# Two decoded rows on one set of partitions, and the mLSTM memory multiplied behind the last weight

## The chip, the cores and the metric

One core of a Trainium2 chip runs the whole program. The metric is device time in microseconds (us) for one execution. Five engines work side by side, each through its own instruction queue: PE (the matrix engine, with its weight loads shown apart as PEld), DVE (elementwise and reductions), ACT (activations and copies), POOL (a second, slower elementwise engine) and SP (no arithmetic; it issues DMAs). SP, ACT and POOL issue DMAs here.

## The reference, cut to what matters

One layer of a hybrid decoder runs on 256 prompt tokens and 8 decoded rows (264 columns in all): a combined projection, a gated recurrence and an mLSTM side by side, an output projection, cross-attention on 256 memory tokens, and a SwiGLU feed-forward. Two pieces of it are touched. The first is the new matrix memory of the prompt's four mLSTM heads:

```
w_end = jnp.exp(bcum[..., -1:] - bcum + li - m_new[..., None])
C_new = dec[..., None, None] * C + jnp.einsum('bhs,bhsd,bhsv->bhdv', w_end, kc, vc)
n_new = dec[..., None] * n + jnp.einsum('bhs,bhsd->bhd', w_end, kc)
```

The prompt's C starts at zero, so for each head the new memory is one product over the 256 tokens, of keys times weights (128 wide) with values and a column of ones (258 wide with padding). It is an output and nothing else in the layer reads it. The second piece is the attention of the 8 decoded rows, which read memory keys and values from a cache, 4 heads of 512 dimensions and 256 memory tokens:

```
s = jnp.einsum('blhd,bmhd->bhlm', xq, mk.astype(dt)).astype(jnp.float32) * (XA_DH ** -0.5)
p = jax.nn.softmax(s, axis=-1).astype(dt)
o = jnp.einsum('bhlm,bmhd->blhd', p, mv.astype(dt)).reshape(B, L, D_MODEL)
```

Each decoded row has keys and values of its own, so these products share no weights between rows.

## The kernel before, in words

The layer is a list `steps` of weight pieces: `w_in`, `w_out`, `w_q`, the memory's `w_k` and `w_v`, `w_o`, and the feed-forward's gate/up and down pieces. Each piece is loaded by SP in halves into one of five `raw` buffers, three pieces ahead. ACT then copies a half in a rounded matmul type into a `w` buffer (four of them), and DVE subtracts that copy from the original: high and low part of the weight. PE multiplies high by high, high by low and low by high, on 264 columns (line `mm<-B,w`). SP's order is the written one; on the other engines a scheduler places instructions by a simulated timeline, except for two stretches that are kept in written order.

Beside this main line run side generators, which `pump` advances between steps: the gates and heads of the mLSTM (`ml_gates`, `ml_prompt`, `ml_values`, `ml_heads`), the memory's norm, and the attentions. A `yield` with a number is a price by which the generators are paced. So their elementwise work stands between the weight splits on DVE and ACT.

In `ml_heads` each head multiplies `kw` (keys times weights) with `vt` (values) into a bank `cps`, 128x258 in plain fp32 and two matmuls for a head. ACT copies it to `cn`, and POOL's queue sends `cn` to the output `o_pc`.

The decode attention is `dec_k` and `dec_v`. A unit is one head and one row: 32 units. `dec_k` loads the row's keys, 128 partitions by 4 chunks of 256 tokens (512 KB), and the values alike, each into a fresh buffer of the pool `B` (26 buffers). The scores are a sum over 512 dimensions: ACT multiplies the first chunk by the query's column, DVE multiplies and adds the other three, ACT and POOL split the result in high and low (`ds`), and PE sums over the partitions by a matrix of ones (`onesr`), two matmuls for a unit, so that each partition holds every score. `dec_v` takes the maximum, the exponential and its sum, and multiplies the four value chunks by the weights with a running sum (`osm`). `NFL` lets two units be in flight.

The last step, `final(15)`, ends with three warm matmuls on ones whose result nobody reads (`warm(3)`). Then come sums of squares (`fin_sums`), the reciprocal root (`rstd_fin`: DVE, ACT's square root, and three more warm matmuls), two transpositions that spread it over the partitions (`spread`), and the products of the output with it, whose results SP and ACT send in nine pieces as `o_y`.

## Time and profile before

| what | before |
|---|---|
| median of 3 runs | 1457.74 us (1456.42 to 1458.74) |
| profiled execution, its own time | 1455.83 us |
| its span | 1454.11 us |
| granted clock of PE, mean | 0.998 |
| PE busy | 1439.2 us, 99% of the span |
| DVE, ACT, POOL busy | 1045.1, 794.9, 128.3 us |
| bytes moved | 326.02 MB, 224 GB/s on the mean |

The span counts from the first to the last instruction. PE's busy time contains overlaps, since matmuls are pipelined and their ends are modelled, so the distance from one start to the next says more of the price of a matmul than its duration. "Idle before, releaser" is the time an engine stood still ahead of a group, with what ended it.

### The profile page before, as it was taken

How to read it: one execution, taken by the hardware profiler on the slowest of the kernel's cores; microseconds unless marked ns; L12 is line 12 of the kernel's file. 1: busy time of each engine (PE TensorE's matmuls, PEld its weight loads, DVE VectorE, ACT ScalarE, POOL GpSimd, SP SyncE). 2: the span in 40 equal slices, each digit the busy share in tenths (PEclk: the TensorE clock that was granted, in tenths of full speed). 3: DMA queues.
4: the chain of work that ended last, by engine and by line, in shares of the span. 5: the costliest groups of instructions: out<-in, count | busy, mean ns of one | idle time of the engine just before them, and what ended most of it. 6: DMA issues, size and time to landing. Idle time of an engine off the chain costs nothing.

```text
span 1454.1 us, 30126 instructions
## 1 busy us (share of the span) xinstructions
PE 1439.2 (99%) x12071; PEld 1415.5 (97%) x12071; DVE 1045.1 (72%) x1999; ACT 794.9 (55%) x1279; POOL 128.3 (9%) x204
## 2 busy tenths in 40 slices
PE   9999999999999999999999999999999999999997
PEld 8999999999999999999999999999999999999997
DVE  7966797898899999987675666555665655565564
ACT  7678685666556666655544444434444443444463
POOL 0001210000124343410000000000000000000000
PEclk9999999999999999999999999999999999999999
DMA  9645896557799877955555555555555555555563
GB/s 288 234 171 179 268 363 231 177 178 271 254 344 355 340 284 297 375 172 192 197 195 194 197 193 201 190 202 190 198 194 196 196 198 194 195 197 192 172 195 112
DMA packets 99757, 326.02 MB, mean 224 GB/s; under 512 B 10944, under 2 KB 19824, under 8 KB 99616
## 3 DMA queue, kind: packets, MB, share of 16 engines
q1 hardware_dynamic: 83616, 269.84, 52.8%
q0 software_dynamic: 15136, 53.16, 10.2%
q8 instruction: 94, 1.54, 0.4%
q10 hardware_dynamic: 864, 1.09, 0.2%
q14 instruction: 47, 0.39, 0.1%
HBM read 312.78 MB, written 11.28 MB: 223 GB/s over the span
## 4 chain that ended last, share of the span: by engine, by line
PE 94%; ACT 2%; DMA 1%; DVE 1%; issue 1%; SPq 0%; POOL 0%; DVEq 0%; POOLq 0%
PE mm L60 90%; PE ax L60 5%; DMA raw<-w_in 1%; ACT B L60 1%; DVE B L60 1%; DMA B<-scr 0%; ACT w L60 0%; DVE w L60 0%; ACT L60 0%; SPq L213 0%; ACT dw L60 0%; DVE ds L60 0%; SPq L1412 0%; DMA scr<-lt 0%; ACT t L60 0%
## 5 line engine op out<-in xcount | busy, mean ns | idle before, releaser
L60 PE MATMUL mm<-B,w 128*128 128x264 f32 (+1 forms) x10960 | 1281.2, 279 | 2.5 <-DVE w L60 2.1
L60 PEld LDWEIGHTS mm<-B,w 128*128 128x128 f32 x10960 | 1260.6, 189 | 10.7 <-DVE w L60 2.4
L60 DVE TENSOR_TENSOR w<-raw,w 128x1024 fp32r<-128x1024 f32 (+1 forms) x522 | 625.4, 1200 | 312.9 <-ACT w L60 312.2
L60 ACT ACTIVATE w<-raw 128x1024 fp32r<-128x1024 f32 (+1 forms) x522 | 536.0, 1028 | 531.8 <-PE mm L60 370.8
L60 PE MATMUL mm<-w,B 128*128 128x512 f32 x384 | 86.5, 380 | 0.0
L60 PEld LDWEIGHTS mm<-w,B 128*128 128x128 f32 x384 | 70.7, 189 | 9.4
L1494 POOL TENSOR_TENSOR B<-B,rstd 128x264 f32<-128x264 f32 x4 | 2.8, 741 | 802.8 <-ACT rstd L60 802.8
L60 DVE TENSOR_TENSOR t<-mm,rstd 128x264 f32<-128x264 f32 x96 | 41.4, 432 | 28.8 <-PE mm L60 28.7
L60 DVE SCALAR_TENSOR_TENSOR B<-B,dw 128x256 f32<-128x256 f32 x128 | 52.2, 461 | 3.2 <-ACT dw L60 2.9
L60 DVE TENSOR_TENSOR xres<-xres,mm 128x264 f32<-128x264 f32 (+1 forms) x81 | 34.2, 424 | 27.2 <-PE mm L60 27.1
L60 DVE SCALAR_TENSOR_TENSOR dw<-B,qsm,dw 128x256 f32<-128x256 f32 x96 | 48.6, 512 | 0.8
L60 PE MATMUL ax<-B,B 128*128 128x256 f32 (+3 forms) x288 | 46.0, 302 | 0.8 <-DVE B L60 0.8
L1162 POOL TENSOR_TENSOR ds<-dw,ds 128x256 fp32r<-128x256 f32 x32 | 36.8, 1151 | 106.9 <-ACT ds L60 104.7
L60 PEld LDWEIGHTS ax<-B,B 128*128 128x128 f32 x288 | 39.9, 191 | 3.0 <-DVE B L60 1.0
L60 ACT ACTIVATE B<-xres,vecs 128x264 fp32r<-128x264 f32 (+1 forms) x64 | 32.1, 502 | 3.5 <-DVE xres L60 1.6
L60 ACT ACTIVATE t<-xres 128x264 f32<-128x264 f32 (+1 forms) x53 | 21.0, 409 | 16.0 <-DVE xres L60 16.0
L1151 POOL DMA_DIRECT2D B<-kcT x32 | 17.4, 544 | 122.8 <-DVE B L60 109.7
L60 DVE SCALAR_TENSOR_TENSOR B<-xres,vecs,B 128x264 fp32r<-128x264 f32 x48 | 23.3, 488 | 4.3 <-ACT B L60 4.3
L60 ACT ACTIVATE dw<-B,qsm 128x256 f32<-128x256 f32 x32 | 16.2, 507 | 16.3 <-issue 6.4
L60 ACT ACTIVATE B<-t 128x264 fp32r<-128x264 f32 (+1 forms) x60 | 24.1, 409 | 1.7 <-DVE t L60 1.5
L60 ACT ACTIVATE dw<-B,B 128x128 f32<-128x128 f32 x64 | 20.9, 390 | 7.1 <-DMA B<-scr 6.3
L60 ACT ACTIVATE dw<-ax,dw 128x256 f32<-128x256 f32 x32 | 15.0, 470 | 17.7 <-DVE dw L60 14.0
(172 smaller groups left out, 691.2 us busy)
## 6 DMA issues: line engine op xcount, KB each, us to landing
raw<-w_gu SPq DMA_DIRECT2D x176, 512.0 KB, 3.6
raw<-w_d SPq DMA_DIRECT2D x80, 512.0 KB, 3.7
raw<-w_in SPq DMA_DIRECT2D x74, 512.0 KB, 5.2
raw<-w_out SPq DMA_DIRECT2D x32, 512.0 KB, 3.8
B<-kcT POOLq DMA_DIRECT2D x32, 512.0 KB, 8.2
raw<-w_q SPq DMA_DIRECT2D x32, 512.0 KB, 5.4
B<-vcT POOLq DMA_DIRECT2D x32, 512.0 KB, 9.1
raw<-w_k SPq DMA_DIRECT2D x32, 512.0 KB, 5.1
```

The source lines that it names most:

```text
L60: return f(*a, **k)
L1151: pool_e.dma_start(kc, kcT[h, b])
L1162: pool_e.tensor_sub(ws[:, 1], acc, ws[:, 0].bitcast(F32))
L1494: e.tensor_mul(st["y"](c), st["y"](c), r)
```

## The change

The first part moves the mLSTM memory. Its eight matmuls, ACT's copies and the output leave `ml_heads`. Keys times weights now stand in one buffer for four heads (`kb`), and this and the two value buffers (`vts`) are written to DRAM by three DMAs of POOL's queue (512, 516 and 516 KB). At the fifth of the last sixteen weight pieces SP reads them back (`state_load`). The matmuls take the place of warm matmuls: head 0 in `final(15)`, head 1 in `rstd_fin`, heads 2 and 3 behind the spread. ACT copies the banks out (`state_out`), and `o_pc` is sent by SP in two halves, the first ahead of the first `o_y`, the second behind the last. PE's order in the last step is now the written one.

The second part puts two decoded rows on one set of partitions: each row takes 64 partitions and 8 chunks instead of 128 and 4, so that 16 units of two rows stand for 32 of one. `onesr` becomes two 64x64 blocks of ones with zeros beside them, and one matmul sums both rows. The queries come on the other partitions by a POOL copy and four DMAs of 64x16 elements for a head (`swap_q`), and results return in the same way (`swap_o`). Keys and values no longer take a fresh buffer for every unit: a `Ring` has two fixed tiles for keys and two for values, and a tile's next load is issued behind its fourth use.

```diff
...
-        warm(3, v[:, 0:1])
+        state_mm((1, 0), (1, 1))
         for k in "ps", "copied":
             fin[k] = bank("ax")
             spread(fin[k], [r[:, j: j + 1] for j in range(3)])
         act.activation(rstd, fin["copied"][:, :N], AF.Copy)
+        state_out(0, act)
+        state_out(1, act)
+        state_mm((2, 0), (2, 1), (3, 0), (3, 1))
+        state_out(2, act)
+        state_out(3, act)
 
...
         return f
 
     hT = {}
+    kept_k = drm.tile([P, H, 2, P], F32, name="kept_k")
+    kept_v = drm.tile([2, P, 2, 2, 258], F32, name="kept_v")
+
+    def state_load():
+        kb, vb, out = B([P, H, 2, P]), [B([P, 2, 2, 258]), B([P, 2, 2, 258])], B([P, H, 258])
+        sp.dma_start(kb, kept_k)
+        for q in range(2):
+            sp.dma_start(vb[q], kept_v[q])
+        fin["state"] = kb, vb, out
+        fin["cps"] = {}
+
+    def state_mm(*parts):
+        kb, vb, out = fin["state"]
+        for h, t in parts:
+            if t == 0:
+                fin["cps"][h] = bank("ax" if h % 2 else "mm")
+            pe.matmul(fin["cps"][h][:, 0:258], kb[:, h, t, :], vb[h // 2][:, t, h % 2, :],
+                      start=t == 0, stop=t == 1)
+
+    def state_out(h, engine):
+        out = fin["state"][2]
+        engine.activation(out[:, h, :], fin["cps"][h][:, 0:258], AF.Copy)
+
 
     def ml_prompt():
         qk = ml["qk"]
         yield STEP
-        kt = B([P, 2, H, P])
+        kt, ml["kb"] = B([P, 2, H, P]), B([P, H, 2, P])
...
-            w = B([P, 1024])
-            E, Pm, kw = w[:, 0:384], w[:, 384:768], w[:, 768:1024]
+            w = B([P, 768])
+            E, Pm, kw = w[:, 0:384], w[:, 384:768], ml["kb"][:, h].rearrange("p t d -> p (t d)")
             ml["w", h] = (Pm, kw)
...
 
     def ml_values():
         vts = [B([P, 2, 2, 258]), B([P, 2, 2, 258])]
+        ml["vts"] = vts
...
-        cn = B([P, H, 258])
...
-            cps = bank("ax")
-            pe.matmul(cps[:, 0:258], kw[:, 0:P], vt[:, 0, :], start=True, stop=False)
-            pe.matmul(cps[:, 0:258], kw[:, P:T], vt[:, 1, :], start=False, stop=True)
-            dps = cps[:, 300:302]
+            dps = bank("ax")[:, 0:2]
             for vb in range(2):
                 act.activation(hh(2 * h + vb)[:, 0:T], nps[:, vb * T: vb * T + T], AF.Copy)
             act.activation(den[:, 3 * h: 3 * h + 2], dps, AF.Abs)
-            act.activation(cn[:, h, :], cps[:, 0:258], AF.Copy)
-        pool_e.dma_start(o_pc, cn)
         yield STEP
 
...
             else:
-                warm(3)
+                state_mm((0, 0), (0, 1))
                 sq = tmp()
...
             if m == 0:
                 act.activation(warm_act, acc_x[:, 0:1], AF.Sqrt)
+            elif m == 4:
+                state_load()
             elif m == KC - 2:
...
             dve.tensor_mul(qsm[:, j, :], p2[:, 1, T - m:], rstd[:, T:N])
             qn["n"] = j + 1
+            if j % 4 == 3:
+                swap_q(j // 4)
             if j == 3:
                 with tc.issue_after(st["split"].ins):
-                    act.activation(onesr, ones, AF.Copy)
+                    act.activation(onesr, ones, AF.Copy, scale=0.0)
+                    for part in (LOW, HIGH):
+                        act.activation(onesr[part, part], ones[part, part], AF.Copy)
                 st["dk"] = side(dec_k(), 5)
                 st["dv"] = side(dec_v(), 4)
         return f
 
     pairs = []
     infl = {"n": 0}
+    NB2 = NS // 2
+    q2 = const.tile([P, H, 2, 4, NB2], F32, name="q2")
+    q3 = const.tile([P, 2, 2, 4, NB2], F32, name="q3")
+    o2, o3 = q2, q3
+    LOW, HIGH = slice(0, 64), slice(64, P)
+
+    by_row = lambda x: x.rearrange("p c (b s) -> p s c b", s=2)
+
+    def swap_q(h):
+        pool_e.tensor_copy(q3[:, h % 2], by_row(qsm[:, 4 * h: 4 * h + 4, :]))
+        for q, part in enumerate((LOW, HIGH)):
+            for e in range(2):
+                pool_e.dma_start(q2[part, h, e], q3[e: P: 2, h % 2, q])
+
+    def swap_o(h):
+        rec = ssm[:, h, 0: NB2]
+        dve.reciprocal(rec, rec)
+        o = o2[:, h].rearrange("p g c b -> p (g c) b")
+        dve.tensor_mul(o, o, rec.rearrange("p (c b) -> p c b", c=1).to_broadcast([P, 8, NB2]))
+        for q, part in enumerate((LOW, HIGH)):
+            for e in range(2):
+                pool_e.dma_start(o3[e: P: 2, h % 2, q], o2[part, h, e])
+        pool_e.tensor_copy(by_row(osm[:, 4 * h: 4 * h + 4, :]), o3[:, h % 2])
+
+    class Ring:
+        def __init__(self, src):
+            self.t, self.at = [B([P, 4, T]), B([P, 4, T])], 0
+            self.src = src.rearrange("h b p c t -> h (b p) c t")
+            self.load()
+            self.load()
+
+        def load(self):
+            u = self.at
+            if u < H * NB2 * 2:
+                self.at = u + 1
+                b = u // 2 % NB2 * 2 * P + u % 2
+                pool_e.dma_start(self.t[u % 2], self.src[u // NS, b: b + 2 * P - 1: 2])
+
+        def __call__(self, j):
+            return self.t[j // 4][:, j % 4, :]
 
     def dec_k():
+        kr = Ring(kcT)
+        st["vr"] = Ring(vcT)
+        yield STEP
         for h in range(H):
             while qn["n"] < 4 * h + 4:
                 yield STEP
-            for b in range(NS):
+            for b in range(NB2):
                 while infl["n"] >= NFL:
                     yield STEP
                 infl["n"] += 1
-                kc = B([P, 4, T])
-                pool_e.dma_start(kc, kcT[h, b])
                 w = sb.tile([P, 264], F32, tag="dw", bufs=2, name=nm("dw"))
                 ws = sb.tile([P, 2, T], F32R, tag="ds", bufs=2, name=nm("ds"))
-                vc = B([P, 4, T])
-                pool_e.dma_start(vc, vcT[h, b])
                 acc = w[:, 0:T]
-                q = [qsm[:, 4 * h + c, b: b + 1] for c in range(4)]
-                act.activation(acc, kc[:, 0, :], AF.Copy, scale=q[0])
-                for c in range(1, 4):
-                    dve.scalar_tensor_tensor(acc, kc[:, c, :], q[c], acc, op0=OP.mult, op1=OP.add)
+                for j in range(8):
+                    q = q2[:, h, j // 4, j % 4, b: b + 1]
+                    if j == 0:
+                        act.activation(acc, kr(0), AF.Copy, scale=q)
+                    else:
+                        dve.scalar_tensor_tensor(acc, kr(j), q, acc, op0=OP.mult, op1=OP.add)
+                    if j % 4 == 3:
+                        kr.load()
+                    if j == 3:
+                        yield 1.0
                 act.activation(ws[:, 0], acc, AF.Copy)
                 pool_e.tensor_sub(ws[:, 1], acc, ws[:, 0].bitcast(F32))
-                pairs.append((h, b, w, vc, ws))
+                pairs.append((h, b, w, ws))
                 yield 1.1
 
     def dec_v():
         done, cur = 0, None
-        while done < H * NS:
+        while done < H * NB2:
             nxt = None
             if pairs:
                 nxt = pairs.pop(0)
                 ps = bank("ax")
-                pe.matmul(by2(ps[:, :T]), onesr, turn(nxt[4][:, 0]), start=True, stop=False)
-                pe.matmul(by2(ps[:, :T]), onesr, turn(nxt[4][:, 1]), start=False, stop=True)
+                pe.matmul(by2(ps[:, :T]), onesr, turn(nxt[3][:, 0]), start=True, stop=False)
+                pe.matmul(by2(ps[:, :T]), onesr, turn(nxt[3][:, 1]), start=False, stop=True)
                 nxt += (ps,)
             cur, todo = nxt, cur
             if todo is None:
                 yield STEP
                 continue
-            h, b, w, vc, _, ps = todo
+            h, b, w, _, ps = todo
             mx, p = w[:, T: T + 1], w[:, :T]
             dve.tensor_reduce(mx, ps[:, :T], axis=AX.X, op=OP.max)
             dve.tensor_scalar(mx, mx, -XSCALE, None, op0=OP.mult)
             act.activation(halves(p), unturn(ps[:, :T]), AF.Exp, scale=XSCALE, bias=mx,
                            accum_out=ssm[:, h, b: b + 1])
             yield 0.5
-            for c in range(4):
-                dve.scalar_tensor_tensor(vc[:, c, :], vc[:, c, :], 1.0, p, op0=OP.mult, op1=OP.mult,
-                                         accum_out=osm[:, 4 * h + c, b: b + 1])
+            for j in range(8):
+                v = st["vr"](j)
+                dve.scalar_tensor_tensor(v, v, 1.0, p, op0=OP.mult, op1=OP.mult,
+                                         accum_out=o2[:, h, j // 4, j % 4, b: b + 1])
+                if j % 4 == 3:
+                    st["vr"].load()
+                if j == 3:
+                    yield 1.0
             infl["n"] -= 1
             done += 1
-            if done % NS == 0:
-                dve.reciprocal(ssm[:, h, :], ssm[:, h, :])
-                for c in range(4):
-                    dve.tensor_mul(osm[:, 4 * h + c, :], osm[:, 4 * h + c, :], ssm[:, h, :])
+            if done % NB2 == 0:
+                swap_o(h)
+                yield STEP
                 st["dh"] = h + 1
             yield STEP
 
...
+        if i == len(steps) - 1:
+            kept.enter_context(tc.manual_schedule(engines={mybir.EngineType.PE}))
...
+        if i == 44:
+            pool_e.dma_start(kept_k, ml["kb"])
+            for q in range(2):
+                pool_e.dma_start(kept_v[q], ml["vts"][q])
     for e, x in pend:
         e(x)
+    kept.close()
     for lo, hi in ((0, 1), (1, 2), (2, 4), (4, 6), (6, 8), (8, 10), (10, 12), (12, 14), (14, 16)):
         for c in range(lo, hi):
             e, r = (pool_e, rstd) if c in POOLC else (dve, fin["ps"][:, :N])
             e.tensor_mul(st["y"](c), st["y"](c), r)
+        if lo == 0:
+            sp.dma_start(o_pc[:, 0:2], fin["state"][2][:, 0:2])
         (act if lo in (1, 4, 8, 12) else sp).dma_start(o_y[:, lo:hi, :], st["y"].tile(lo // 4)[:, lo % 4: lo % 4 + hi - lo, :])
+    sp.dma_start(o_pc[:, 2:4], fin["state"][2][:, 2:4])
```

On PE, in the last head of `ml_heads`, the rows before are these (`ax` with number 2083 is the bank `cps`, `B_1626` the buffer with keys times weights, `B_1889` the values):

```order
L60 MATMUL ax_2078<-B_1889,B_1626 128x256
L60 MATMUL ax_2078<-B_1889,B_1626 128x128
L60 MATMUL ax_2083<-B_1626,B_1889 128x258 x2
L60 MATMUL ax_2083<-ones,B_1889 128x1 x3
L60 MATMUL mm_2128<-B_148,w_2006 128x264
```

and at the same place of the changed kernel:

```order
L60 MATMUL ax_2082<-B_1893,B_1630 128x256
L60 MATMUL ax_2082<-B_1893,B_1630 128x128
L60 MATMUL ax_2087<-ones,B_1893 128x1 x3
L60 MATMUL mm_2129<-B_152,w_2010 128x264
L60 MATMUL mm_2129<-B_153,w_2010 128x264
```

The two matmuls of 258 columns are gone, and the weight's next matmul stands directly behind the three sums.

On PE, from the last weight matmuls to the end of the program, before (`c` is the small tile of the reciprocal root, `ident` the identity of the spread):

```order
L60 MATMUL mm_17732<-B_16571,w_17683 128x264
L60 MATMUL mm_17769<-ones 128x128 x3
L60 MATMUL ax_17728<-ones,t_17773 128x1 x3
L60 MATMUL mm_17791<-ones,c_17782 128x128 x3
L60 MATMUL ax_17795<-ident,c_17783 128x128 x2
L60 MATMUL ax_17795<-ident,c_17783 128x8
L60 MATMUL ax_17799<-ident,c_17783 128x128 x2
L60 MATMUL ax_17799<-ident,c_17783 128x8
```

and of the changed kernel (`B_17018` holds `kept_k`, `B_17019` and `B_17020` the halves of `kept_v`):

```order
L60 MATMUL mm_17545<-B_16375,w_17494 128x264
L60 MATMUL mm_17582<-B_17019,B_17018 128x258 x2
L60 MATMUL ax_17539<-ones,t_17585 128x1 x3
L60 MATMUL ax_17603<-B_17019,B_17018 128x258 x2
L60 MATMUL ax_17606<-ident,c_17595 128x128 x2
L60 MATMUL ax_17606<-ident,c_17595 128x8
L60 MATMUL ax_17610<-ident,c_17595 128x128 x2
L60 MATMUL ax_17610<-ident,c_17595 128x8
L60 MATMUL mm_17617<-B_17020,B_17018 128x258 x2
L60 MATMUL ax_17620<-B_17020,B_17018 128x258 x2
```

Heads 0 and 1 stand where the warm matmuls stood, heads 2 and 3 behind the spread.

On DVE, early in the decode attention, before (`dw` is a unit's scores, `B_5470` its keys, the rows with `w` are weight splits):

```order
L60 TENSOR_TENSOR w_5488<-raw_5374,w_5488 128x8x128
L60 SCALAR_TENSOR_TENSOR dw_5472<-B_5470,qsm,dw_5472 128x256
L60 TENSOR_SCALAR dw_5388<-dw_5388 128x1
L60 SCALAR_TENSOR_TENSOR dw_5472<-B_5470,qsm,dw_5472 128x256 x2
L60 TENSOR_TENSOR w_5570<-raw_5456,w_5570 128x8x128
L60 SCALAR_TENSOR_TENSOR B_5390,osm<-B_5390,dw_5388 128x256 x4
```

and of the changed kernel, at one of the closest places between two uses of a key tile (`B_5225` and `B_5226` are the two key tiles of the ring, `q_117` the turned queries):

```order
L60 SCALAR_TENSOR_TENSOR dw_7242<-B_5226,q_117,dw_7242 128x256
L60 TENSOR_TENSOR w_7715<-raw_7624,w_7715 128x1024
L60 SCALAR_TENSOR_TENSOR dw_7467<-B_5225,q_117,dw_7467 128x256
L60 TENSOR_TENSOR w_7768<-raw_7690,w_7768 128x1024
L60 SCALAR_TENSOR_TENSOR dw_7467<-B_5226,q_117,dw_7467 128x256 x2
L60 TENSOR_TENSOR w_7771<-raw_7692,w_7771 128x1024
```

The first row is unit `dw_7242`'s last use of the second key tile, which is then loaded again; the fifth row is the next unit's first use of it. Two weight splits and one product stand between them. Before, every unit's keys have a buffer of their own.

On SP, the end of the queue of the changed kernel; before, only the `o_y` rows stand there:

```order
L1581 DMA o_pc<-B_17021 128x516
L1582 DMA o_y<-B_16806 128x264
L1582 DMA o_y<-B_16806 128x528
L1582 DMA o_y<-B_17016 128x528
L1582 DMA o_y<-B_17232 128x528
L1582 DMA o_y<-B_17441 128x528
L1583 DMA o_pc<-B_17021 128x516
```

The two halves of the new memory enclose the five pieces of the output.

## The prediction

> **What bounds the kernel now.** I read the page's busy shares and slices first, then the waits of PE.
>
> ```profile
> span 1454.1 us, 30126 instructions
> PE 1439.2 (99%) x12071; PEld 1415.5 (97%) x12071; DVE 1045.1 (72%) x1999; ACT 794.9 (55%) x1279; POOL 128.3 (9%) x204
> PE mm L60 <- DVE w L60: 2.1, 2, 1.9
> PE ax L60 <- ACT w L60: 2.1, 3, 1.5
> PE mm L60 <- DVE ones L60: 1.1, 1, 1.1
> PE ax L60 <- DVE B L60: 0.8, 1, 0.8
> ```
>
> PE is busy for 99% of the span, and its named waits (total, times, longest) are about 6 us in all. So the kernel is a row of matmuls, and a matmul taken out of the dense part is worth its distance to the next start, as long as the weights still arrive in time. The span is 1454.11 us and the profiled execution 1455.83, so 1.72 us lie around it; the execution stands 1.91 us under the median of 1457.74.
>
> Next are the stretch of the decode attention, by windows (start:end, length, busy times of PE, PEld, DVE, ACT and POOL, clock, share of the DMA engines, GB/s), and a stretch of the feed-forward for comparison:
>
> ```profile
> 398.00:625.00 227.00, 227.00 (x1468) 210.87 (x1466) 220.02 (x564) 144.55 (x271) 88.95 (x121) 1.00 0.87 326
> 735.00:1000.00 265.00, 265.00 (x2358) 265.00 (x2357) 158.17 (x192) 115.81 (x133) 0.00 (x0) 1.00 0.56 195
> ```
>
> PE never waits in the decode stretch, but DVE is busy for 220.02 of 227 us. It has 7 us to spare there, and 107 of 265 in the feed-forward. That scarcity is where this change can go wrong.
>
> **What the matmuls that go are worth.** Starts and lengths of groups on PE, in the mLSTM and in the decode attention:
>
> ```profile
> 165.73 1.03 PE L60 MATMUL ax<-B,B 128*128 128x258 f32 x4
> 166.60 0.72 PE L60 MATMUL ax<-ones,B 128*128 128x1 f32 x6
> 461.81 0.28 PE L60 MATMUL ax<-ds,onesr 128*128 128x256 f32 x1
> 461.93 2.78 PE L60 MATMUL mm<-B,w 128*128 128x512 f32 x16
> L60 PE MATMUL ax<-B,B 128*128 128x258 f32 x16 | 4.2, 388 | 0.8 <-DVE B L60 0.8
> L60 PE MATMUL ax<-ds,onesr 128*128 128x256 f32 x64 | 17.1, 277 | 0.0
> ```
>
> A head's new memory is four records, from 165.73 to the next group's start at 166.60: 0.87 us, and four heads 3.5. A sum over the ones takes from 461.81 to 461.93, 0.12 us (0.11 where I averaged neighbouring starts). 64 become 32: 32 x 0.115 = 3.65 us. Both stand in stretches in which PE hardly waits, and the order on PE around them stays, so I take both whole: -7.15 us. The first heads wait for DVE's `B` (0.8 us in the row); that wait belongs to the keys and stays. ACT's four copies `cn` and POOL's `o_pc` go without worth, as ACT is busy for 55%.
>
> **What DVE and ACT get in the decode attention.** Groups between 375 and 655 us (count, busy, mean ns, idle before):
>
> ```profile
> L60 DVE TENSOR_TENSOR w<-raw,w 128x1024 fp32r<-128x1024 f32 x94 | 120.7, 1287 | 10.8 <-ACT w L60 10.5
> L60 DVE SCALAR_TENSOR_TENSOR dw<-B,qsm,dw 128x256 f32<-128x256 f32 x96 | 48.6, 512 | 0.8
> L60 DVE SCALAR_TENSOR_TENSOR B<-B,dw 128x256 f32<-128x256 f32 x128 | 52.2, 461 | 3.2 <-ACT dw L60 2.9
> L60 DVE TENSOR_REDUCE dw<-ax 128x1 f32<-128x256 f32 x32 | 13.3, 416 | 0.3 <-PE ax L60 0.2
> L60 DVE TENSOR_SCALAR dw<-dw 128x1 f32<-128x1 f32 x32 | 4.7, 147 | 0.2
> L60 ACT ACTIVATE w<-raw 128x1024 fp32r<-128x1024 f32 x94 | 99.0, 1055 | 39.5 <-PE mm L60 30.5 <-issue 5.1 <-DMA raw<-w_v 2.1
> L60 ACT ACTIVATE dw<-B,qsm 128x256 f32<-128x256 f32 x32 | 16.2, 507 | 16.3 <-issue 6.4 <-DVE B L60 4.7 <-ACT w L60 2.9
> L1162 POOL TENSOR_TENSOR ds<-dw,ds 128x256 fp32r<-128x256 f32 x32 | 36.8, 1151 | 106.9 <-ACT ds L60 104.7
> L1151 POOL DMA_DIRECT2D B<-kcT x32 | 17.4, 544 | 122.8 <-DVE B L60 109.7
> ```
>
> The multiply-adds on keys go from 96 to 112 (8 chunks for 16 units, less ACT's first): +16 x 0.512 = +8.2 us. Value products stay 128. Maxima and scalings halve: -16 x (0.416 + 0.147) = -9.0 us, and 16 small products at the heads' ends become four, at about the scaling's price, -12 x 0.147 = -1.8. DVE gains 2.6 us in all. ACT loses half of its first products (-16 x 0.507 = -8.1 us) and half of its copies and exponentials besides. POOL's subtractions fall by 16 x 1.151 = 18.4 us; its 32 new small DMAs cost 32 issues of 0.544 us, 17.4. None of this is on PE's path by itself, and it counts zero. What hides it is that the splits run ahead as far as their four buffers allow: ACT's copies stand idle for 30.5 us until PE releases a buffer, against 2.1 for a weight's DMA. If that cover went, every late us of DVE would be a us of PE.
>
> **The turned queries and results.** Each head's queries go through a POOL copy, four DMAs of 4 KB and their landing. The trace has no such small transfer on this queue; the nearest is a full key tile alone, at 3.8 us (below). For the first head this delays the first unit by 0 to 6 us, and later heads' queries are ready ahead. The attention ends some 24 us earlier in the changed order against PE's weight steps, which pays for the return of the results too. I take 0.
>
> **The ring.** Landing times, issue to data, of the 512 KB transfers (KB each, median us), of two single key tiles, at 581 us with nothing ahead of it and at 596.8 with several, and of the outputs in this stretch:
>
> ```profile
> raw<-w_d SPq DMA_DIRECT2D x80, 512.0 KB, 3.7
> raw<-w_v SPq DMA_DIRECT2D x32, 512.0 KB, 6.8
> B<-kcT POOLq DMA_DIRECT2D x30, 512.0 KB, 8.4
> B<-kcT POOLq DMA_DIRECT2D x1, 512.0 KB, 3.8
> ...
> B<-kcT POOLq DMA_DIRECT2D x1, 512.0 KB, 9.9
> ...
> o_k<-t POOLq DMA_DIRECT2D x16, 128.0 KB, 6.2
> o_v<-B POOLq DMA_DIRECT2D x8, 256.0 KB, 4.9
> ```
>
> Before, each unit had buffers of its own, and loads ran ahead. Now a tile is loaded behind its last use, and has until its next use. I added up DVE's durations from the trace over the changed order between these two points, for 61 reloads. Most have 9 to 20 us; fourteen have 2.9 to 7.9, nearly all of the second key tile. The place in the order shown above has two splits and one product: 2 x 1.287 + 0.512 = 3.1 us, 3.6 with the issue. The shortfall, summed over the reloads, is 4 us if a tile lands in 5, 11 at 6.5, 22 at 7.5 and 38 at 8.7. Against it stand DVE's 7 us and the 2.6 it gains. The ends are thus 0 (at 5, the tile alone) and 28 (at 8.7). I take a landing of 6.3, nearer the tile alone, because the second key tile is mostly asked for 2 to 7 us behind the last value tile and not in bursts of six. The shortfall is then about 10 us, DVE's spare is 9.6, and I count +1 us for the unevenness.
>
> The rate that the stretch needs: the weights' 195 GB/s (row of the feed-forward), 60 tiles (31.5 MB) of keys and values in about 218 us, 144, and the memory's keys and values written out (16 x 128 and 8 x 256 KB), 19: 358. One slice of 36 us of the page reached more:
>
> ```profile
> GB/s 288 234 171 179 268 363 231 177 178 271 254 344 355 340 284 297 375 172 192 197 195 194 197 193 201 190 202 190 198 194 196 196 198 194 195 197 192 172 195 112
> ```
>
> The slice with 375 says that the DMA can carry it, with 4% left. The Trainium skill, page "DMA: Bandwidth & Descriptors", section "Specifications", puts the limit of HBM for a core at about 358 GB/s, and this would leave nothing and keep landings at their burst level; by that rule the time would be the first rival's. The slice of 375 disagrees with the figure, so I keep the row.
>
> **The state's way through DRAM.** POOL's three writes (1.57 MB) stand on a queue whose engine is busy for 9% of the span. SP's three reads stand between weight loads of the last step's piece 4, where a weight half lands in 3.7 us and the DMA is at 56%. At 396 GB/s (the tail's row below) they take 4 us. SP runs as far ahead as five half buffers allow: a down piece of 12 chunks has 36 matmuls of 265 / 2358 = 0.112 us, 4.05 us, so two and a half pieces are 10 us, and 4 more on a queue that needs 3.7 still fit. I take 0, with 0 to 1.4 us as bounds (4 + 2 x 3.7 for two halves behind all three, less 10).
>
> **The tail.** The chain after the last weight matmul, from the timeline, and two windows of its end:
>
> ```profile
> 1441.56 0.83 PE L60 MATMUL mm<-ones 128*128 128x128 f32 x6
> 1442.45 0.83 PE L60 MATMUL ax<-ones,t 128*128 128x1 f32 x6
> 1443.32 0.16 DVE L60 TENSOR_SCALAR c<-ax 128x3 f32<-128x3 f32 x1 [1.06 <-PE ax L60]
> 1443.52 0.20 ACT L60 ACTIVATE c<-c 128x3 f32<-128x3 f32 x1 [0.51 <-DVE c L60]
> 1444.57 1.41 PEld L60 LDWEIGHTS ax<-ident,c 128*128 128x128 f32 x12 [0.29 <-DVE c L60]
> 1445.90 4.71 SPq L1495 DMA_DIRECT2D o_y<-B  x5
> 1448.00:1450.00 2.00, 0.00 (x0) 0.00 (x0) 1.61 (x5) 0.00 (x0) 1.44 (x3) 0.92 1.03 387
> 1450.00:1452.50 2.50, 0.00 (x0) 0.00 (x0) 0.00 (x0) 0.00 (x0) 0.00 (x0) 0.50 1.04 396
> ```
>
> Head 0 takes 0.87 us from 1441.56 and ends at 1442.43, when the sums start at 1442.45. Head 1 fits between the sums' end, 1443.3, and the spread at 1444.57. ACT copies head 0 out at about 1443.0 to 1443.45, just ahead of the square root at 1443.52. These cost 0, at most 0.2. Heads 2 and 3 run behind the spread, on a PE that has nothing else. The DMA then is saturated from 1448 to 1452.5. The first half of `o_pc` (264 KB) is asked for some 1 us ahead of the first `o_y`, while the DMA idles: 0. The second is last in the queue: 264 KB at 396 GB/s, +0.67 us. Bounds: 0, and 1.36 if both halves wait behind the output.
>
> **Sum.** 1455.83 - 3.5 - 3.65 + 1.0 (ring) + 0.67 (last half) = 1450.35 for the profiled execution; on the median, 1.91 higher, 1452.3, 0.38% less than before.
>
> **Rivals.**
>
> 1. *The ring's tiles come late* (slower; 0.25). DVE stands at the first use of a tile, the splits behind it on DVE come late, and PE with them. For it: DVE's 97%, the median landing of 8.4, 358 GB/s. Against it: single tiles at 3.8. It decides for "slower" when the loss passes 9.5 us, at a landing of about 7.3 (19 us of shortfall less 9.6); at 8.7 the loss is 28, 1479. Middle: about 1462.
> 2. *The tail pays more* (0.12). State copies delay the square root and ACT's share of the output's DMAs, and both halves queue: +2 to +3 us instead of 0.67, about 1454.
> 3. *PE's gain comes back as waits* (0.08). The splits run at DVE's pace in the decode stretch, so PE waits for the us that it saves there: only the mLSTM's 3.5 us stay or less, 1455 to 1458. Against it: 5 us of split slack, and DVE gains 2.6 of the 3.65.
>
> **How the numbers follow.** My forecast has 0.55 and its own range is 1449.5 to 1454.8: the low end is the sum without ring and tail, 1455.83 + 1.91 - 7.15 = 1450.6, less 1.1 for scatter of the medians; the high end adds a us or two of ring and tail. The whole range takes in rivals 2 and 3 and the lower half of the first, to 1464. A measurement of this kernel tells about 0.2%, 2.9 us, from no change. Faster: 0.53 from the forecast, 0.08 from rival 2, 0.01 from the others, 0.62. Same: 0.02, 0.04, 0.06, and 0.04 from a ring that loses 4 to 9 us, 0.16. Slower: 0.22, nearly all the ring's.
>
> **What would show it.** The two groups of matmuls must be gone, the mLSTM ending about 3.5 us earlier and the first feed-forward step 6 to 7. Right on the ring: PE without waits from 375 to 655, key tiles landing in about 6 us, and DVE with little idle ahead of `dw<-B,q` products. Wrong: DVE idle released by `B<-kcT` and PE waiting for `w`. The tail is right if the span behind the last weight matmul is 0.5 to 1 us longer.

## The result, and the profile after

The changed kernel takes 1482.31 us (median of 4 runs, 1478.93 to 1484.0) against 1457.55 us of the kernel before beside it (4 runs): a ratio of 1.0169, with a 95% interval of 1.0157 to 1.0182. It is slower by 25 us where I forecast 5 us faster. The profiled execution took 1482.38 us, its span is 1480.7.

First the page of the changed kernel, then its waits of PE over the whole span (total, times, longest):

```profile
span 1480.7 us, 29940 instructions
PE 1444.0 (98%) x12027; PEld 1413.9 (95%) x12027; DVE 1046.7 (71%) x1971; ACT 773.6 (52%) x1217; POOL 134.2 (9%) x230
```

```profile
PE ax L60 <- ACT ds L60: 8.0, 5, 4.6
PE mm L60 <- DVE w L60: 5.2, 6, 1.9
PE ax L60 <- DVE B L60: 4.0, 3, 1.7
PE mm L60 <- DVE t L60: 3.5, 1, 3.5
PE ax L60 <- POOL ds L1236: 2.7, 3, 1.6
```

PE's busy time has hardly moved; its waits have grown from some 7 to 29 us. Where they stand is told by comparing the two traces matmul by matmul. Both have the same 11,344 matmuls on weights, so the n-th of one answers to the n-th of the other. The changed kernel is 1.7 us ahead when the decode attention begins (at 375 us), 25.7 behind when it ends (at 660), and 25.7 behind at the last weight matmul. These rows show the lead at 303 us (303.25 - 301.58), and then the last weight matmul, each of before and then of the changed kernel:

```profile
303.25 0.59 PE L60 MATMUL ax<-lt,ones 128*128 128x256 f32 x2
```

```profile
301.58 0.59 PE L60 MATMUL ax<-lt,ones 128*128 128x256 f32 x2
```

```profile
1441.14 0.58 PE L60 MATMUL mm<-B,w 128*128 128x264 f32 x3
```

```profile
1466.82 0.58 PE L60 MATMUL mm<-B,w 128*128 128x264 f32 x3
```

From 660 us on nothing more is lost until the last weight: 1466.82 - 1441.14 = 25.68. What follows the last weight matmul is 0.88 us longer. So the span's 26.6 us are -1.7 (start and mLSTM), +27.4 (decode attention) and +0.9 (tail).

The decode stretch of the changed kernel, by windows as in the prediction, then its groups on DVE and ACT (count, busy, mean ns, idle before them), then its DMA issues (KB each, median us to landing):

```profile
398.00:625.00 227.00, 206.19 (x1290) 187.38 (x1290) 202.85 (x513) 111.37 (x191) 82.05 (x128) 0.98 0.87 302
```

```profile
L60 DVE SCALAR_TENSOR_TENSOR dw<-B,q,dw 128x256 f32<-128x256 f32 x112 | 58.4, 527 | 24.5 <-DMA B<-kcT 17.1 <-ACT dw L60 6.8 <-DVE w L60 0.2
L60 DVE SCALAR_TENSOR_TENSOR B<-B,dw 128x256 f32<-128x256 f32 x128 | 54.1, 483 | 1.8 <-DMA B<-vcT 1.1 <-ACT dw L60 0.6
L60 ACT ACTIVATE dw<-B,q 128x256 f32<-128x256 f32 x16 | 8.2, 510 | 43.4 <-DMA B<-kcT 22.8 <-DVE B L60 10.3 <-DVE w L60 4.8
```

```profile
B<-kcT POOLq DMA_DIRECT2D x30, 512.0 KB, 7.3
B<-vcT POOLq DMA_DIRECT2D x30, 512.0 KB, 6.2
```

PE, which was never idle there, is busy for 206 of 227 us. DVE waits 17.1 us for key tiles, and ACT 22.8 more. Key tiles land in a median 7.3 us, less than the 8.4 of before. So they are not slower; they are asked for later.

One such wait from end to end, in the changed kernel's timeline of DVE, POOL, ACT, DVE and PE (start, length, engine, work, idle before it and what ended it):

```profile
548.67 0.47 DVE L60 SCALAR_TENSOR_TENSOR dw<-B,q,dw 128x256 f32<-128x256 f32 x1
...
552.55 0.54 POOL L1206 DMA_DIRECT2D B<-kcT  x1 [7.84 <-ACT w L60]
...
561.60 0.51 ACT L60 ACTIVATE dw<-B,q 128x256 f32<-128x256 f32 x1 [7.57 <-DMA B<-kcT]
562.01 0.40 ACT L60 ACTIVATE ds<-dw 128x256 fp32r<-128x256 f32 x1
562.32 1.04 ACT L60 ACTIVATE w<-raw 128x1024 fp32r<-128x1024 f32 x1
...
562.21 1.36 DVE L60 SCALAR_TENSOR_TENSOR dw<-B,q,dw 128x256 f32<-128x256 f32 x2 [3.98 <-ACT dw L60]
...
562.46 0.58 PE L60 MATMUL ax<-ds,onesr 128*128 128x256 f32 x1 [4.62 <-ACT ds L60]
```

DVE's last product on the first key tile ends at 549.14. POOL asks for the next keys only at 552.55, 3.4 us later (its row names a weight split on ACT as what it waited for; which need of the load that stands for was not settled), and they land after 8.9 us more. Of the 30 reloads, 24 are asked for within 0.7 us of the last product on their tile, and six 1.1 to 3.4 us behind it. ACT stands for 7.57 us before its product on it. Behind that product in ACT's queue are the copy `ds` of the unit before, for which PE stands 4.62 us, and the next weight split. So ACT's wait for one unit's keys holds up another unit's sums.

### The profile page after: what moved, and what is told of

Same layout as the page of the kernel before. It is cut to its first block, busy times and chain, and to the rows that moved or that the text cites. A ratio compares the mean times of both kernels' runs of the same rounds, so it can differ in the third digit from the quotient of the medians.

```text
span 1480.7 us, 29940 instructions
## 1 busy us (share of the span) xinstructions
PE 1444.0 (98%) x12027; PEld 1413.9 (95%) x12027; DVE 1046.7 (71%) x1971; ACT 773.6 (52%) x1217; POOL 134.2 (9%) x230
## 4 chain that ended last, share of the span: by engine, by line
PE 57%; DMA 1%; DVE 1%; issue 0%; DVEq 0%; ACT 0%
PE mm L60 56%; PE ax L60 1%; DMA B<-vcT 1%; DMA B<-kcT 1%; DVE B L60 0%; DVE w L60 0%; DVE dw L60 0%; DVE c L60 0%; DVEq L1667 0%; DVE t L60 0%; ACT c L60 0%; DVEq L60 0%
## 5 line engine op out<-in xcount | busy, mean ns | idle before, releaser
L60 DVE SCALAR_TENSOR_TENSOR dw<-B,q,dw 128x256 f32<-128x256 f32 x112 | 58.4, 527 | 24.5 <-DMA B<-kcT 17.1
L60 ACT ACTIVATE dw<-B,q 128x256 f32<-128x256 f32 x16 | 8.2, 510 | 43.4 <-DMA B<-kcT 22.8
L60 ACT ACTIVATE dw<-B,B 128x128 f32<-128x128 f32 x64 | 20.7, 392 | 12.8 <-DMA B<-scr 11.2
L60 PE MATMUL ax<-B,w 128*128 128x264 f32 x144 | 22.2, 281 | 2.1 <-ACT w L60 2.0
L60 PEld LDWEIGHTS ax<-B,w 128*128 128x128 f32 x144 | 19.3, 189 | 3.2 <-ACT w L60 3.0
```

Of the source, the lines that this page charges most:

```text
L60: return f(*a, **k)
```

## Experiments

The theories are RING (two key tiles leave no time to land), RATE (the DMA can't carry the shorter stretch), SWAP (the small DMAs of queries and results clog POOL's queue) and, later, SCORES (too few score tiles). "Decode stretch" below is the difference to before between 375 and 660 us, matmul by matmul.

**e1, the first part alone.**

The decode attention is that of before, with one row for a unit and a buffer for every unit. The mLSTM memory, `state_load`, `state_mm`, `state_out` and `o_pc` are as in the change.

> Only the first part: the mLSTM memory behind the last weight matmul; the decode attention is that of before. By the alignment of the two traces (equal weight matmuls compared) this part gains 1.7 us in the mLSTM and loses 0.9 behind the last weight matmul, the decode attention has the whole loss: 1456.8 us, ratio 0.9995. If instead the DRAM traffic of the state were what disturbs the decode stretch, this kernel would be slower than before by some us.

Measured: 1455.7 us, ratio 0.9991 (0.9981 to 1.0). The mLSTM gains 4.1 us, the decode stretch loses 1.55 although its code is the same (the order shifted a little), and the tail loses 0.89. PE's waits between 375 and 655 us are a single row:

```profile
PE ax L60 <- POOL ds L1187: 0.2, 1, 0.2
```

The state's way through DRAM does not cost the decode stretch its 27 us; the loss is the second part's.

**e2, fresh tiles for every unit.**

```diff
-        kr = Ring(kcT)
-        st["vr"] = Ring(vcT)
...
+                kc = [half(kcT, h, b, u) for u in range(2)]
+                vc = [half(vcT, h, b, u) for u in range(2)]
```

> Both parts, but each unit of two rows takes fresh tiles of the pool for its keys and values and asks for all four at once at its start, as before; the ring of two tiles is gone. Theory RING (two key tiles leave no time to land): the 27 us of the decode stretch vanish and the 3.65 us of the sums come through, 1451 to 1457 us. Theory RATE (the DMA can't carry keys, values and weights in the shorter stretch): no better than 1475. Theory SWAP (the small DMAs and copies of the turned queries hold POOL's queue): no better than 1475.

Measured: 1468.36 us, 1.0083 (1.0067 to 1.01). Half of the loss comes back, and the decode stretch still loses 15 us. The forecast of RING is missed by 11 us. Nine of them are one stall, in the waits of PE, and its cause is in POOL's timeline:

```profile
PE ax L60 <- POOL ds L1223: 9.1, 1, 9.1
```

```profile
454.42 0.53 POOL L1191 DMA_DIRECT2D q<-q  x1 [1.73 <-DMA B<-kcT]
456.98 0.52 POOL L1191 DMA_DIRECT2D q<-q  x1 [2.03 <-DMA B<-kcT]
459.54 0.52 POOL L1191 DMA_DIRECT2D q<-q  x1 [2.04 <-DMA B<-vcT]
...
469.79 0.55 POOL L1182 DMA_DIRECT2D q<-q  x1 [1.96 <-DMA B<-vcT]
...
471.51 0.74 POOL L1223 TENSOR_TENSOR ds<-dw,ds 128x256 fp32r<-128x256 f32 x1
```

Eight small DMAs of 4 KB each wait 1.5 to 2.3 us, seven of them for an older key or value load by their rows, and the subtraction that PE needs stands behind them. The loads themselves are slow here: asked for in bursts, eight of them land one every 2.55 us, 12 to 20 us after their issue, while the DMA engines are busy for 63% of the time (462 to 472 us, 237 GB/s). So fresh tiles do not cure the lateness; they bring another wait. Here SWAP is right: with many loads in flight the small DMAs are held. In the changed kernel's ring there are few loads in flight, and this wait is short.

**e3, four key tiles.**

```diff
-            self.t, self.at = [B([P, 4, T]), B([P, 4, T])], 0
+            self.t, self.at, self.used = [B([P, 4, T]) for _ in range(n)], 0, 0
...
-        kr = Ring(kcT)
-        st["vr"] = Ring(vcT)
+        kr = Ring(kcT, 4)
+        st["vr"] = Ring(vcT, 2)
```

> Both parts, the ring of keys with four tiles instead of two, that of values with two as it is. RING, with keys the short side: 1452 to 1460 us. RATE and SWAP: no better than 1475.

Measured: 1462.21 us, 1.0038 (1.0025 to 1.005). Two more key tiles give back 20 of the 25 us, which ends 2 us above RING's range. DVE's and ACT's waits for key tiles are gone; DVE still waits 4.5 us for value tiles (waits, 375 to 655 us):

```profile
DVE B L60 <- DMA B<-vcT: 4.5, 5, 1.3
```

**e4, no transfers between partitions.**

```diff
-        for q, part in enumerate((LOW, HIGH)):
-            for e in range(2):
-                pool_e.dma_start(q2[part, h, e], q3[e: P: 2, h % 2, q])
+        pool_e.tensor_copy(q2[:, h], q3[:, h % 2])
...
+        pool_e.tensor_copy(o3[:, h % 2], o2[:, h])
```

> Both parts with the ring as it is; the eight small DMAs of a head that carry queries and results between partitions are replaced by one POOL copy each way, so that queries and results stay on their partitions (this move is left out of the computation). SWAP: 10 us or more come back, 1472 or less. RING and RATE: 1478 to 1483.

Measured: 1488.08 us, 1.0209 (1.0193 to 1.0226). Taking the small DMAs away does not help with a ring of two; it costs 6 us, which no theory had. So SWAP is not the cause here. Its waits for key tiles are as long as the changed kernel's (25.1 us on DVE and 15.4 on ACT, 40.5 against 39.9). PE stands 23.5 us between 375 and 655 against 20.7, and its granted clock is lower, 0.95 against 0.98 in this stretch:

```profile
398.00:625.00 227.00, 203.37 (x1234) 183.51 (x1233) 194.31 (x514) 105.93 (x186) 72.21 (x110) 0.95 0.83 288
```

PE's longer waits and the slower clock behind them (see the section on the hardware) are enough for its 6 us; why it has more pauses stays open.

**e5, e7 and e8, three score tiles.** All three have `bufs=3` for `dw` and one temporary `t` less, for the space; e5 with four key tiles, e7 with two, e8 on the first part alone.

```diff
-    NB, NT, NL, NFL = 26, 6, 3, 2
+    NB, NT, NL, NFL = 26, 5, 3, 2
...
-tag="dw", bufs=2
+tag="dw", bufs=3
```

> Both parts, four key tiles as in e3, and three score tiles (dw) instead of two; for the space the pool of temporaries t has five tiles instead of six. Theory SCORES: what is left in e3 is ACT's first product of a unit, which waits until the value products of two units before have released their score tile, with weight splits queued behind it; then the 3.4 us stall of PE near 597 us and most of the 7.5 us that the decode stretch still loses go: 1452 to 1458 us. If that stall is only the order's chance: 1460 to 1464.

> Both parts, the ring of two key tiles as it is, with three score tiles and five temporaries. RING: the key tiles still come late, 1474 us or more. SCORES as the main cause: 1465 or less.

> The first part alone (as e1) with three score tiles and five temporaries: the decode attention of before, which has a buffer for every unit. If score tiles bind only the units of two rows, the same as e1: 1455 to 1457 us.

Measured: e5 1466.53 us, 1.0066 (1.0051 to 1.0081); e7 1480.3, 1.0161 (1.0146 to 1.0176); e8 1470.18, 1.0091 (1.0076 to 1.0106). e7 says that score tiles are not the main cause. e5 and e8 missed: three score tiles make the decode attention of before 14 us slower too, so e5 proves nothing against SCORES by itself.

**e6, nothing is loaded again.**

```diff
-            if u < H * NB2 * 2:
+            if u < 2:
```

> Both parts with the ring of two, but each ring tile is loaded once and never again; all units use the first unit's keys and values (the other rows' attention is left out). Takes away every wait for a key tile and 31 MB of traffic. RING: the loss that the reloads cause goes, and what SCORES holds stays, 1455 to 1464 us. If the order of the coarser units on DVE were the cause, and not the tiles: 1475 or more.

Measured: 1457.16 us, 1.0002 (0.9993 to 1.0012). The decode stretch is at -0.33 us instead of +27.4: the whole loss hangs on the reloads. But the 3.65 us of the sums do not show in it either, though no tile is waited for. By the distances from each start to the next, the 64 sums cost 7.3 us before and the 32 of e6 cost 4.1, so nearly the whole is saved there. The other matmuls of the stretch cost 2.9 us more, and PE's waits (375 to 655 us; before had none) name 1.8 of them:

```profile
PE ax L60 <- POOL ds L1236: 1.4, 2, 0.7
PE mm L60 <- DVE w L60: 0.4, 1, 0.4
```

(At this kernel's very end stand 4.8 us more than before with neither transfers nor work, against 0.9 in the others; I have no cause for that. The stretch's number does not contain them.)

**e9 to e12, the control for the score tiles.** e9 is e5 with six temporaries `t` and two `lt`; e10 has a third value tile besides; e11 is e9 with a pause after every two chunks; e12 is the first part alone with e9's pools. The first lines are the pools of all four, the last the pause of e11.

```diff
-    NB, NT, NL, NFL = 26, 6, 3, 2
+    NB, NT, NL, NFL = 26, 6, 2, 2
...
-                    if j == 3:
-                        yield 1.0
+                    if j in (1, 3, 5):
+                        yield 0.5
```

> As e5 (four key tiles, three score tiles), but all six temporaries t; the space comes from the pool lt, which the mLSTM uses (two tiles instead of three). e8 says that five tiles t or three score tiles cost the decode stretch 14 us by themselves; this tells which. If the t tiles did it, SCORES can be judged here: 1452 to 1458 us, with e3's stall of 3.4 us gone. If the third score tile itself upsets the order: 1465 or more.

> As e9 with a third value tile. e3's DVE stood 4.5 us for value tiles. If they still cost PE time: 1 to 4 us less than e9. If the rest is the order's: the same within 3 us.

> As e9, with a pause of the generators after every two chunks of keys and of values instead of one after four (the same total price). If blocks of eight value products (4.3 us of DVE in a row) are what makes splits late: 2 to 5 us less than e9. If not: the same within 3 us.

> The first part alone with three score tiles and two tiles lt, all six tiles t: the control for e9. If the t tiles cost e8 its 14 us: as e1, 1455 to 1457. If the third score tile did: 1466 or more.

Measured: e9 1464.53 us, 1.0053 (1.0038 to 1.0068); e10 1463.56, 1.0044 (1.0027 to 1.0061); e11 1462.49, 1.004 (1.0025 to 1.0055); e12 1470.12, 1.0094 (1.0079 to 1.0109). e9 lies between its two forecasts, half a us from that of the third score tile. The temporaries are not it: the first part alone is 14 us slower also in e12, with the third score tile and two `lt`. ACT's first products in e1, and then in e12, show where:

```profile
L60 ACT ACTIVATE dw<-B,qsm 128x256 f32<-128x256 f32 x31 | 15.7, 508 | 22.4 <-issue 9.4 <-DVE B L60 5.3 <-DMA B<-kcT 3.1
```

```profile
L60 ACT ACTIVATE dw<-B,qsm 128x256 f32<-128x256 f32 x31 | 15.7, 507 | 41.1 <-DMA B<-kcT 19.6 <-issue 14.1 <-DVE B L60 5.0
```

With a third score tile ACT's product stands earlier against the data: it waits 19.6 us for keys (3.1 in e1). That is the same wait as in the changed kernel, got in another way. It is a reading of the two traces; the order itself was not pinned to prove it. The finer pauses of e11 (2.0 us less than e9) and the value tile of e10 (1.0 us less) are no clear difference beside it: the intervals overlap with e9's, and neither decides between its two forecasts.

**e13, four key and three value tiles, two score tiles.** Against e3:

```diff
-        st["vr"] = Ring(vcT, 2)
+        st["vr"] = Ring(vcT, 3)
```

> Four key tiles, three value tiles, two score tiles: e3 with one value tile more and nothing else. If e3's rest hangs on the value tiles (DVE stood 4.5 us for them): 1454 to 1459 us. If it is in the order of ACT and DVE: 1460 to 1464, as e3.

Measured: 1455.17 us, 0.9988 (0.9979 to 0.9998): the only kernel here whose interval lies below 1. One value tile takes away 7 us of e3's. The decode stretch, by windows, and what is left of DVE's and ACT's waits for tiles between 375 and 655 us:

```profile
398.00:625.00 227.00, 224.00 (x1415) 205.64 (x1414) 221.71 (x568) 127.19 (x222) 91.26 (x142) 1.00 0.91 324
```

```profile
DVE B L60 <- DMA B<-vcT: 0.5, 1, 0.5
...
ACT dw L60 <- DMA B<-kcT: 2.6, 1, 2.6
```

The DMA moves 324 GB/s here, against 302 in the changed kernel. So the rate was not the limit.

**e14 and e15, no reloads of keys, and of values.**

```diff
-            if u < H * NB2 * 2:
+            if u < (2 if self.name == 'k' else H * NB2 * 2):
```

This is e14; e15 has `'v'` in the place of `'k'`.

> The ring of two and two, keys loaded once for all units (the other rows' scores are left out), values as they are. If keys are the main cause, as e3 says: 20 us or more less than the changed kernel, 1456 to 1463 us.

> The counterpart: values loaded once for all units (the other rows' results are left out), keys as they are. If keys are the main cause: 1472 us or more, although a quarter of the stretch's bytes is gone, which also speaks against RATE. If the rate of bytes were the cause: as e14.

Measured: e14 1458.11 us, 1.0006 (0.9996 to 1.0016); e15 1471.56, 1.0098 (1.0083 to 1.0113), 0.4 us under its forecast; decode stretch +4.8 and +18.1. Keys account for 23 of the 27 us, values for 9 (together more than the whole, as the same us can hang on both). In e15 the stretch needs far less of the DMA, and DVE and ACT still wait for keys (windows, then waits):

```profile
398.00:625.00 227.00, 214.35 (x1353) 195.64 (x1353) 212.09 (x564) 119.19 (x213) 72.49 (x108) 0.98 0.75 246
```

```profile
ACT dw L60 <- DMA B<-kcT: 14.1, 4, 5.1
DVE dw L60 <- DMA B<-kcT: 10.3, 5, 3.0
```

At 246 GB/s, where before moved 326, RATE is out.

**e16, the second part alone with the tiles of e13.** The mLSTM memory, `final(15)`, `rstd_fin` and the tail are as before; the ring has four and three tiles.

```diff
...
+        kr = Ring(kcT, 4)
+        st["vr"] = Ring(vcT, 3)
```

> The second part alone with four key and three value tiles; the mLSTM memory as before. If PE's saved sums come through once the tiles are there: 1453.5 to 1455 us. If they come back as waits between DVE and ACT, as e13's decode stretch says: 1457 to 1459 us, and e13's gain is all the first part's.

Measured: 1460.32 us, 1.0024 (1.0014 to 1.0034), a little worse than the worse case. The decode stretch is at +3.0 us. So e13's gain belongs to the first part, and two rows on shared partitions gave nothing with any number of tiles tried. Part of the 3.0 us is one pause of PE of 2.08 us with a slow clock behind it (rows in the section on the hardware).

## Why the prediction was wrong

- **The ring (+1 us taken, +27.4 measured for the whole stretch).** This is the step that failed; it was the first rival, with 0.25, whose worst case of 1479 was still too low. The mechanism of that rival was right; my sum was wrong in three ways. First, I took a landing of 6.3 us "nearer the tile alone"; the median is 7.3. My own table has some 20 us of shortfall there. Second, I counted the time until DVE's next use. ACT makes each unit's first product and uses the tile earlier, and its 22.8 us of waiting stood nowhere in the working. I had put nearly all the short times at the second key tile; five of the eleven waits for keys, and more than half of their 39.9 us, were ACT's for the first. Third, I set the shortfall against DVE's spare time of 9.6 us as if it could be spread. The waits come in whole pieces of up to 7.6 us, on two queues that keep their order, and hold up the splits behind them; the spare time lies elsewhere.
- **The rate.** 358 GB/s was a need that never arose, as the stretch got longer. e13, which loses little, ran at 324. The weighing of the limit against the slice of 375 decided nothing: the rival came true by latency, at a lower rate than before (302 against 326).
- **The turned queries (0).** e4, without their transfers, is not faster, so no run shows a cost of theirs with the ring of two.
- **The sums (-3.65 us).** The stretch as a whole did not get shorter by them in any run: -0.33 with no reloads at all (e6), +1.25 in e13, +3.0 in e16. The sums themselves got cheaper (7.3 us before, 4.1 in e6), and the matmuls between them dearer, 2.9 us in e6. This was the third rival, at 0.08. In that stretch PE runs without a wait in the kernel before, but DVE is busy for 97% of it, and as I read it a PE that asks earlier is made to wait. PE's named waits in the stretch are 1.8 us in e6, 2.8 in e13 and 3.3 in e16; the rest is not traced, and e1, which keeps all 64 sums, also loses 1.55 us. (The product in my working, 32 x 0.115, is 3.68; the 0.03 change nothing.)
- **The mLSTM (-3.5 us).** It is -4.1 in e1, -1.7 in the changed kernel, and between -1.3 and -4.1 in the others with the first part, so the size was about right where nothing got in its way. In the changed kernel ACT waited 3.4 us for a scratch load (0.8 before), and PE 1.5 more behind that. A new write of 516 KB stands ahead of that load on POOL's queue; I had counted POOL's writes at nothing, for their issue on POOL, and not what is queued behind them. That the write is the cause is not shown: in e1 it stands at the same place, and ACT waited 1.6 us. The rows are ACT's waits between 150 and 175 us, before and after:

```profile
ACT dw L60 <- DMA B<-scr: 0.8, 1, 0.8
```

```profile
ACT dw L60 <- DMA B<-scr: 3.4, 1, 3.4
```

- **The tail (+0.67 us).** Measured +0.88, and 0.87 to 0.90 in nearly every kernel with the first part. The mechanism was right and the size 0.2 low: the second half of `o_pc` lands 0.70 us behind the last piece of the output, which lands as long after the last weight matmul as before. ACT's copies did not delay the square root: it stands 2.38 us behind the start of the last three weight matmuls in both (1443.52 - 1441.14 before, 1469.20 - 1466.82 after, ACT's row below). The second rival fell.

```profile
1469.20 0.20 ACT L60 ACTIVATE c<-c 128x3 f32<-128x3 f32 x1 [0.23 <-DVE c L60]
```

- **The state's reads (0).** Right: the whole feed-forward stays at the same distance of 25.68 us.

## What to carry to other kernels

A buffer that is loaded again behind its last use needs, from there to its next use on any engine, issue plus landing. Count that for the first engine that touches it, one interval at a time, and not as a sum against idle time. Where matmuls are taken out of a stretch in which the other engines have no time left, first ask what PE would run into next. A mixed change is worth taking apart: here one part was worth 1 to 2 us and the other cost 27.

## What the runs showed of the hardware

A stall of PE can cost about half as much again behind it. These windows of the changed kernel hold the two longest stalls, of 4.6 and 3.6 us, and a short one of 1.7 between 535 and 539 (the last three numbers are the granted clock, the share of the DMA engines and GB/s):

```profile
535.00:539.00 4.00, 2.27 (x14) 1.76 (x13) 3.23 (x11) 1.22 (x3) 0.00 (x0) 1.00 0.92 375
...
557.00:562.00 5.00, 0.84 (x5) 0.49 (x3) 1.22 (x2) 0.40 (x1) 0.00 (x0) 0.97 0.97 324
562.00:566.00 4.00, 3.54 (x16) 3.54 (x17) 3.73 (x8) 2.60 (x6) 1.39 (x3) 0.50 0.81 319
566.00:570.00 4.00, 4.00 (x23) 3.87 (x22) 2.51 (x7) 2.16 (x6) 0.52 (x1) 0.69 0.87 289
...
619.00:623.00 4.00, 0.84 (x6) 0.52 (x4) 2.52 (x5) 0.00 (x0) 0.00 (x0) 1.00 0.24 99
623.00:625.00 2.00, 1.61 (x5) 1.46 (x6) 2.00 (x5) 0.39 (x1) 0.59 (x1) 0.53 0.69 195
625.00:627.00 2.00, 2.00 (x10) 1.70 (x9) 2.00 (x6) 2.00 (x7) 1.48 (x2) 0.62 0.57 215
```

After the pause of 4.6 us, which ends at 562.46, the clock is at 0.50 up to 566 and at 0.69 for 4 us more: with PE's busy time, 3.54 x 0.50 + 4 x 0.31 = 3.0 us lost behind it. After the one of 3.6 us it is 1.61 x 0.47 + 2 x 0.38 = 1.5. The pause of 1.7 us left the clock at 1.00. The Trainium skill, page "TensorE: Matmul & The Clock Gate", section "HAM oscillation — how this bites in real kernels", gives the rule that PE should have no gaps over about 3.4 us; these rows agree with it. Not every trace does, and there the measurement decides. In e16 a pause of 2.08 us was followed by a clock of 0.57, in e4 one of 1.92 us by the same (461 to 465 us), while one of 2.17 us in e9 left it at 1.00 (602 to 606 us). What tells them apart is open. The rows of e16:

```profile
545.10 0.38 PE L60 MATMUL ax<-ds,onesr 128*128 128x256 f32 x1 [2.08 <-POOL ds L1215]
...
546.00:550.00 4.00, 4.00 (x18) 3.50 (x17) 3.31 (x10) 2.76 (x6) 1.53 (x3) 0.57 0.93 297
```

POOL's DMAs wait for each other. In e2, small ones stood about 2 us each for loads issued earlier. The trace shows POOL's DMAs using eight semaphores in turn. Each of the eight small ones was issued 0.3 to 0.6 us after the landing of the DMA eight places ahead of it, and by its record waits for that one's semaphore. So my reading is that an issue waits for the DMA eight places ahead; no run varied that alone.
